# An encoder's attention taken by pairs of heads: softmax weights kept in float32, products with v in two column halves of the array, sums on GpSimd

## The chip, the core and the metric

The kernel runs on one core of a Trainium2 chip. The core has a matrix engine (TensorE, PE in the profile, with its weight loads as PEld), a vector engine (VectorE, DVE), an activation engine (ScalarE, ACT), GpSimd (POOL) and a queue for transfers (SyncE, SP). The metric is device time in microseconds of one execution. Everything is to be computed to float32 accuracy.

## What is computed

Two layers of an encoder over 1024 tokens of 1024 features. The first layer mixes tokens by multi-head latent attention (8 heads) and by retention, side by side, the second by gated linear attention; both end with a gated MLP. The change lies in the attention of the first layer: scores of every head, a softmax over all 1024 keys, and the product with v.

```python
def _mla(cq, ckv, k_rope, positions, q_norm, kv_norm, w_uq, w_ukv, q_head_norm, k_head_norm):
    ...
    scale = MLA_QK ** -0.5                       # 8 heads, 96 columns of q and k, 64 of v
    nb = S // Q_BLOCK
    qb = q.reshape(B, nb, Q_BLOCK, H, MLA_QK).transpose(1, 0, 2, 3, 4)

    def block(qi):
        s = jnp.einsum('bqhd,bkhd->bhqk', qi, k).astype(jnp.float32) * scale
        p = jax.nn.softmax(s, axis=-1).astype(v.dtype)
        return jnp.einsum('bhqk,bkhe->bqhe', p, v)
    ...

for layer in range(DEPTH):                       # DEPTH = 2
    if layer % 2 == 0:
        h = _rmsnorm(x, mix_norm_even[i])
        cq, ckv, k_rope, rq, rk, rv, rg = _split(h @ w_in_even[i], EVEN_SPLIT)
        a = _mla(cq, ckv, k_rope, positions, ...)
        r = _retention(rq, rk, rv, rg, positions, ...)
        x = x + jnp.concatenate([a, r], axis=-1) @ w_out_even[i]
    else:
        ...                                      # gated linear attention
    x = x + _conv_ffn(x, ...)
```

## The kernel before

Work is recorded by Python generators; a scheduling layer then orders each engine's instructions. `weave(main, n, side, m)` steps a main generator and m of n steps of a side one in proportion, and so fixes what lies beside what. A matmul is nearly always a split one: a float32 operand is kept as two float32r parts, hi (a copy on ScalarE) and lo (a subtraction on VectorE, or on GpSimd where `split` is told so), and `mm3` (L346 to L352) issues hi*hi, hi*lo and lo*hi. The matmul line is L349 for all of them. Products that stay in plain float32 (L1385, L811, L1077) are one instruction in the program and two records in the trace.

The attention is the class `Mla`. `produce(pr)` makes q, k and v of a pair of heads from the compressed projections, in 128-token tiles; v is split into hi and lo pages of 128 columns, 64 of v and 64 constants (1.0 in hi, 0.0 in lo), so that one product gives the output and the sum of the weights at once. `prepare(i)` turns q and k of head i to features by tokens, splits them, and finds each query's largest score: 16 matmuls of hi parts (L1440), a maximum on VectorE for each (L1441), and a row that subtracts it. `attend(i)` runs one head: 2 halves of 512 queries by 8 key tiles of 128. A step is one `mm3` for the scores, an exponential on ScalarE (L1469), the split of the weights x into hi and lo (cast on ScalarE, L327, subtraction on VectorE, every second one on GpSimd, L328), and, four steps behind (AHEAD), one `mm3` with the v page into an accumulating PSUM bank. After 8 key tiles ScalarE copies 64 rows of output and VectorE 64 rows of the sum; after the second head of a pair, `y = 1/z` by Ln and Exp with one Newton step, the division, and a DMA to DRAM, from which the output projection reads it back.

The order around it: the retention of the last pair of heads (`ret(3)`) has as its side work the gates, `produce(0)` and `prepare(0)`; then come eight loops of `attend(i)`, with `prepare(i + 1)`, and `produce` of the next pair in the even ones, as side work; in the last two, the operands of the output projection are loaded (`early`) and its first weights (`weights`). PSUM has 8 banks: 5 in the lane "mm" and 3 in the lane "mr", which the side work uses. SBUF pages come in tags with a number of buffers each: "w" has 6 pages of 4 KB, "raw" 2, "hx" 32, "pg" 3.

## Time and profile before

| | |
|---|---|
| median of 3 runs | 2590.84 us (2588.73 to 2591.42) |
| profiled execution | 2591.09 us, span 2589.3 us |
| PE busy | 2551.8 us (99%) |
| DVE busy | 1650.5 us (64%) |
| ACT busy | 1187.7 us (46%) |
| POOL busy | 151.0 us (6%) |

A row of a group gives line, engine, operation, the tiles it writes and reads (`out<-in`), the shape, a count, the busy time in us, the mean of one in ns, and the engine's idle time before them with what ended it. Records of matmuls overlap, since they are pipelined: the time that one costs is read from the starts of successive ones, in a timeline, and not from its length. A shape such as 128*64 128x512 is rows*columns of the array and then partitions x elements of the output. In a timeline the columns are the start, the time until the last of the group ends, engine, line, operation, tiles, shape and count.

### The profile page before, as it was taken

The numbers are of one execution on the slowest core, as the hardware profiler recorded it, in microseconds if no ns is written. First come the engines' busy times: TensorE is split into PE (matmuls) and PEld (weight loads), VectorE is DVE, ScalarE is ACT, GpSimd is POOL, SyncE is SP. The second block draws the span as 40 slices with busy tenths as digits, with TensorE's granted clock in tenths as the row PEclk, the third lists the DMA queues.
The fourth block names the chain that finished last, engine by engine and source line by source line (L and its number), as shares of the span: only waits on it lengthen the run. The fifth ranks groups of instructions, "written<-read, shape, count | busy, mean of one in ns | idle before, by whom it ended". The sixth has DMA issues, their size and how long they took to land.

```text
span 2589.3 us, 33133 instructions
## 1 busy us (share of the span) xinstructions
PE 2551.8 (99%) x12776; PEld 2134.4 (82%) x12776; DVE 1650.5 (64%) x2607; ACT 1187.7 (46%) x2163; POOL 151.0 (6%) x222
## 2 busy tenths in 40 slices
PE   8999999999999999999999999999999999999999
PEld 8889877777888888887888898897788888887887
DVE  6444778778678767676363455648588676775331
ACT  5333667788444333334242445657453333334221
POOL 0000024343000000000000000000000000000000
PEclk9999999999999999999999999999999999999999
DMA  6111100003632222227453211223722222237443
GB/s 193 40 45 42 42 23 12 18 18 122 195 98 73 82 86 85 82 95 262 151 153 106 62 50 45 70 68 108 256 88 75 87 84 82 82 114 254 139 142 92
DMA packets 320596, 253.81 MB, mean 98 GB/s; under 512 B 14828, under 2 KB 271957, under 8 KB 320437
## 3 DMA queue, kind: packets, MB, share of 16 engines
q1 hardware_dynamic: 317877, 243.30, 30.1%
q0 software_dynamic: 2560, 8.39, 0.8%
q8 instruction: 100, 1.64, 0.3%
q14 instruction: 59, 0.48, 0.1%
HBM read 193.71 MB, written 57.93 MB: 97 GB/s over the span
## 4 chain that ended last, share of the span: by engine, by line
PE 71%; DVE 5%; ACT 3%; DMA 3%; issue 1%; SPq 0%; DVEq 0%; ACTq 0%
PE mm L349 65%; DMA st<-d 1%; PE mr L1098 1%; PE mr L349 1%; PE mr L1028 1%; PE mr L1385 1%; DVE hx L328 1%; PE mr L1440 1%; PE mr L1073 1%; PE mr L1387 1%; ACT w L327 1%; DVE sr L1441 0%; DVE xa L1145 0%; DVE hr L998 0%; DVE w L328 0%
## 5 line engine op out<-in xcount | busy, mean ns | idle before, releaser
L349 PE MATMUL mm<-hx,w 128*128 128x512 f32 (+1 forms) x3600 | 869.4, 393 | 1.5 <-ACT hx L1237 1.4
L349 PEld LDWEIGHTS mm<-hx,w 128*128 128x128 f32 (+1 forms) x3600 | 669.9, 187 | 145.4 <-ACT hx L1237 2.2
L328 DVE TENSOR_TENSOR w<-raw,w 128x1024 fp32r<-128x1024 f32 (+2 forms) x271 | 299.3, 1107 | 300.3 <-ACT w L327 284.8
L327 ACT CAST w<-raw 128x1024 fp32r<-128x1024 f32 (+2 forms) x321 | 285.6, 893 | 414.0 <-PE mm L349 351.7
L349 PE MATMUL mm<-w,hx 128*128 128x256 f32 (+1 forms) x2304 | 363.2, 305 | 2.5 <-POOL w L328 1.9
L349 PE MATMUL mm<-h,wf 128*128 128x512 f32 x1368 | 328.9, 389 | 0.0
L349 PEld LDWEIGHTS mm<-w,hx 128*128 128x128 f32 x2304 | 307.3, 191 | 22.6 <-POOL w L328 2.5
L349 PE MATMUL mm<-gh,w 128*128 128x512 f32 x1344 | 316.4, 393 | 4.9 <-ACT gh L327 3.9
L349 PEld LDWEIGHTS mm<-gh,w 128*128 128x128 f32 x1344 | 251.3, 189 | 62.2 <-ACT gh L327 5.6
L349 PEld LDWEIGHTS mm<-h,wf 128*128 128x128 f32 x1368 | 256.8, 188 | 53.3
L1235 DVE TENSOR_TENSOR hx<-mm,hx 128x512 f32<-128x512 f32 x190 | 130.5, 687 | 154.3 <-PE mm L349 154.3
L327 ACT CAST wf<-raw 128x1024 fp32r<-128x1024 f32 x78 | 81.9, 1053 | 187.3 <-DVE raw L1221 118.1
L349 PE MATMUL mm<-hx,wf 128*128 128x512 f32 x552 | 131.9, 389 | 0.0
L349 PEld LDWEIGHTS mm<-hx,wf 128*128 128x128 f32 x552 | 103.6, 188 | 21.5
L349 PE MATMUL mm<-h,w 128*128 128x512 f32 x456 | 109.5, 389 | 0.0
L349 PE MATMUL mm<-hr,hr 128*128 128x512 f32 x336 | 103.8, 402 | 2.3 <-ACT hf L1469 1.7
L328 DVE TENSOR_TENSOR wf<-raw,wf 128x1024 fp32r<-128x1024 f32 x78 | 95.1, 1222 | 12.0 <-ACT wf L327 11.9
L349 PEld LDWEIGHTS mm<-h,w 128*128 128x128 f32 x456 | 85.6, 188 | 17.8
L1265 ACT ACTIVATE pg<-pg 128x1024 f32<-128x1024 f32 x44 | 46.7, 1062 | 106.3 <-DVE pg L1264 105.8
L1264 DVE SCALAR_TENSOR_TENSOR pg<-mm,c,pg 128x512 f32<-128x512 f32 (+1 forms) x100 | 74.0, 746 | 33.0 <-ACT pg L1259 33.0
L349 PE MATMUL mm<-hf,w 128*128 128x512 f32 x384 | 88.8, 392 | 0.0
L349 PEld LDWEIGHTS mm<-hf,w 128*128 128x128 f32 x384 | 72.2, 188 | 16.0
(364 smaller groups left out, 3084.6 us busy)
## 6 DMA issues: line engine op xcount, KB each, us to landing
raw<-in_ffn_w_up SPq DMA_DIRECT2D x88, 512.0 KB
raw<-in_ffn_w_down SPq DMA_DIRECT2D x64, 512.0 KB
st<-d SPq DMA_DIRECT2D x95, 256.0 KB
d<-pg SPq DMA_DIRECT2D x44, 512.0 KB
raw<-in_ffn_w_down SPq DMA_DIRECT2D x32, 384.0 KB
raw<-in_w_in_odd SPq DMA_DIRECT2D x24, 512.0 KB
raw<-in_w_out_even SPq DMA_DIRECT2D x16, 512.0 KB
raw<-in_w_out_odd SPq DMA_DIRECT2D x16, 512.0 KB
```

Of the source, the lines that this page charges most:

```text
L327: self.nc.scalar.copy(hi, src)
L328: return (rest or self.nc.vector).tensor_tensor(lo, src, hi.bitcast(F32), ALU.subtract)
L349: mm = lambda w, x, start, stop: self.nc.tensor.matmul(out, lhsT=w, rhs=x, start=start, stop=stop, skip_group_check=more)
L1028: nc.tensor.matmul(ps[:, n], lhsT=k3[:, t % 4], rhs=vt(t), start=True, stop=True)
L1073: nc.tensor.matmul(p[:, blk(j)], lhsT=kc[:, blk(j)], rhs=qc[:, blk(j)], start=True, stop=True)
L1098: nc.tensor.matmul(ps, lhsT=w[:, blk(t % 4)], rhs=x, start=n == 0, stop=n == len(terms) - 1)
L1235: add = lambda out, x, y: nc.vector.tensor_tensor(out, x, y, ALU.add)
L1264: nc.vector.scalar_tensor_tensor(dst, g[hf][:, src], cw(tap), dst, ALU.mult, ALU.add)
L1265: nc.scalar.activation(cv, cv, AF.Silu)
L1385: nc.tensor.matmul(ps[:, :192], lhsT=e.cq[k][hf][:, blk(t % 4)], rhs=w1[:, k], start=k == 0, stop=k == 2)
L1387: nc.tensor.matmul(ps[:, 256:], lhsT=e.ckv[k][hf][:, blk(t % 4)], rhs=w2[:, k], start=k == 0, stop=k == 1)
L1440: nc.tensor.matmul(ps, lhsT=qs.tok(0, t)[0], rhs=ks.hi[0][hf], start=True, stop=True)
```

## The change

Attention goes by pairs of heads. `attend(pr)` holds both heads in one step: two `mm3` of scores, two exponentials into one page x of 128 x 2 x 512 in float32 (tag "w"), and no split. GpSimd adds x into `acc` in every step but the first of a half. `products` runs four key tiles at a time: for each, two float32 matmuls with 64 columns of v as weights, head 0 into partitions 0 to 63 of a bank and head 1 into 64 to 127, that is, into the two column halves of the array. `divide` sums `acc` over the partitions by two float32 matmuls with 64 columns of ones, two steps after the half's last products, and divides. v is one float32 page without constants. `prepare(1)` moves in front of the loop, beside the retention of the last pair; in the loop of pair p lie `produce(p + 1)`, `prepare(2p + 2)` and `prepare(2p + 3)`; in the last loop the output projection's operands and its first weights. The weights of `produce` move from "w" to "raw" pages, and every second head's split q and k to "hx".

```diff
--- before.py
+++ after.py
@@ -703,7 +703,7 @@
                 yield from g
             for g in each[-2:]:
                 yield next(g)
-            for i, _ in enumerate(many(m.produce(0), m.prepare(0))):
+            for i, _ in enumerate(many(m.produce(0), m.prepare(0), m.prepare(1))):
                 yield
                 if i in RG:
                     yield next(each[RG.index(i) - 2])
@@ -730,20 +730,12 @@
 
         rest = many(mixed(proj_qk(3), norms()), rg(0, 1, 2, 3))
         self.weave(ret(2), 19, islice(rest, W2), W2)
-        self.weave(ret(3), 19, rest, 39 - W2)
-        for i in range(8):
-            side, n = [], 0
-            if i < 7:
-                side.append(self.on((1, 1), m.prepare(i + 1)))
-                n += 13
-            if i % 2 == 0 and i < 6:
-                side.append(self.on((0, 1), m.produce(i // 2 + 1)))
-                n += 10
-            if i >= 6:
-                side.append(self.on((1, 0), many(early(0, 4, 5, 6, 7, 0, 1)) if i == 6 else
-                                    many(early(0, 2), weights(), early(1, 4, 5, 6, 7, 0, 1, 2))))
-                n += 6 if i == 6 else 9
-            self.weave(m.attend(i), 2 * NT - 2 * (i < 6), many(*side), n)
+        self.weave(ret(3), 19, rest, 52 - W2)
+        for p in range(3):
+            side = many(self.on((0, 1), m.produce(p + 1)), *(self.on((1, 1), m.prepare(2 * p + j)) for j in (2, 3)))
+            self.weave(m.attend(p), 2 * NT - 1, side, 36)
+        side = many(early(0, 4, 5, 6, 7, 0, 1, 2), early(1, 4, 5, 6, 7, 0, 1, 2), weights())
+        self.weave(m.attend(3), 2 * NT, self.on((1, 0), side), 15)
         outs = [(o_a[p], None) for p in range(4)] + [(o_r[p], gates[p]) for p in range(4)]
         return outs, *o, w, [], first[0]
 
@@ -1357,13 +1349,13 @@
         self.e, self.nc, self.outs, self.parts = e, e.nc, outs, parts
         self.wq = e.io["mla_w_uq"][0].rearrange("(k p) f -> p k f", p=P)
         self.wkv = e.io["mla_w_ukv"][0].rearrange("(k p) f -> p k f", p=P)
-        self.pair, self.head, self.behind = {}, {}, []
+        self.pair, self.head, self.behind, self.later = {}, {}, [], []
 
     def produce(self, pr):
 
         e, nc = self.e, self.nc
         krr, krs = e.kr
-        w1, w2 = (e.page(s, F32, "w") for s in ([P, 3, 192], [P, 2, 256]))
+        w1, w2 = (e.page(s, F32, "raw") for s in ([P, 3, 192], [P, 2, 256]))
         nc.sync.dma_start(out=w1, in_=self.wq[:, :, blk(pr, 192)])
         nc.sync.dma_start(out=w2, in_=self.wkv[:, :, blk(pr, 256)])
         qp, kp, vp = [], [], []
@@ -1377,9 +1369,8 @@
                 if not c:
                     qp.append(e.page([P, 2, 192], tag="hx"))
                     kp.append(e.page([P, 2, 192], tag="hx"))
-                    vp.append([e.page([P, 2, 2, P], F32R, tag="hx") for _ in range(2)])
-                    for v, x in zip(vp[-1], (1.0, 0.0)):
-                        nc.gpsimd.memset(v[:, :, :, 64:].bitcast(F32), x)
+                if t % 4 == 0:
+                    vp.append(e.page([P, 4, 2, 64], tag="hx"))
                 ps = e.bank()
                 for k in range(3):
                     nc.tensor.matmul(ps[:, :192], lhsT=e.cq[k][hf][:, blk(t % 4)], rhs=w1[:, k], start=k == 0, stop=k == 2)
@@ -1390,7 +1381,7 @@
                     junk = e.half([P, P])
                     nc.scalar.activation(junk[:, :96], ps[:, blk(j, 96)], AF.Square, accum_out=st[:, t % 4, j:j + 1])
                     nc.scalar.activation(junk[:, :64], pk[:, j, :64], AF.Square, accum_out=st[:, t % 4, 2 + j:3 + j])
-                e.split(pk[:, :, 64:], *(v[:, c, :, :64] for v in vp[-1]))
+                nc.scalar.copy(vp[-1][:, t % 4], pk[:, :, 64:])
                 nc.vector.tensor_copy(qp[-1][:, c], ps[:, :192])
                 nc.vector.tensor_copy(heads(kp[-1][:, c], 96)[:, :, :64], pk[:, :, :64])
                 yield
@@ -1418,7 +1409,7 @@
         e, nc = self.e, self.nc
         qp, kp, _ = self.pair[i // 2]
         hc = blk(i % 2, 96)
-        qs, ks = e.new_split(1), e.new_split(1)
+        qs, ks = (e.new_split(1, "hx" if i % 2 else None) for _ in range(2))
         for t in qs.hi[0] + qs.lo[0] + ks.hi[0] + ks.lo[0]:
             nc.gpsimd.memset(t[96:].bitcast(F32), 0.0)
         for hf in range(2):
@@ -1450,57 +1441,67 @@
         self.head[i] = qs, ks
         yield
 
-    def attend(self, i):
+    def attend(self, pr):
 
         e, nc = self.e, self.nc
+        two = [self.head.pop(2 * pr + j) for j in range(2)]
         for hf in range(2):
-            q, pa = qs.half(0, hf), e.bank()
+            acc = e.page([P, 2, H2])
             for kt in range(NT):
...
+                x = e.page([P, 2, H2], F32, "w")
+                for j, (qs, ks) in enumerate(two):
+                    ps = e.bank()
+                    e.mm3(ps, ks.tok(0, kt), qs.half(0, hf), True, True)
+                    nc.scalar.activation(x[:, j], ps, AF.Exp, scale=96 ** -0.5)
+
+                if kt:
+                    nc.gpsimd.tensor_tensor(acc, acc if kt > 1 else self.behind[-1][2], x, ALU.add)
+                self.behind.append((hf, kt, x))
                 if len(self.behind) > AHEAD:
-                    self.product(*self.behind.pop(0))
-                yield
-        while self.behind and i == 7:
-            self.product(*self.behind.pop(0))
-            yield
-
-    def product(self, i, hf, kt, pa, both):
+                    self.products(pr if kt else pr - (not hf), acc if kt else self.acc)
+                if self.later and kt == 2:
+                    self.later.pop()()
+                yield
+            self.acc = acc
+        if pr == 3:
+            self.products(pr, acc)
+            yield
+            self.later.pop()()
+            yield
+
+    def products(self, pr, acc):
+
         e, nc = self.e, self.nc
...
+        for hf, kt, x in [self.behind.pop(0) for _ in range(AHEAD)]:
+            if not kt:
+                self.pa = e.bank()
+            v = self.pair[pr][2][kt // 4]
+            for j in range(2):
+                nc.tensor.matmul(self.pa[blk(j, 64)], lhsT=v[:, kt % 4, j], rhs=x[:, j], start=kt == 0, stop=kt == NT - 1)
         if kt < NT - 1:
             return
...
+        oy = e.page([P, 2, H2])
+        nc.scalar.copy(oy[:, 0], self.pa)
+        self.later.append(lambda: self.divide(pr, hf, acc, oy[:, 0], oy[:, 1]))
+
+    def divide(self, pr, hf, acc, o, y):
+
+        e, nc = self.e, self.nc
+        z, ps = e.half(), e.bank()
+        for j in range(2):
+            nc.tensor.matmul(ps[blk(j, 64)], lhsT=e.ones[:, :64].bitcast(F32), rhs=acc[:, j], start=True, stop=True)
+        nc.scalar.activation(y, ps, AF.Ln)
+        nc.scalar.activation(y, y, AF.Exp, scale=-1.0)
+        nc.vector.scalar_tensor_tensor(z, ps, -1.0, y, ALU.mult, ALU.mult)
+        nc.vector.scalar_tensor_tensor(y, z, 2.0, y, ALU.add, ALU.mult)
+        nc.vector.tensor_tensor(o, o, y, ALU.mult)
+        if not hf:
+            self.outs[pr] = e.waiting()
+        if pr == 3 and not hf:
+            self.parts[pr] = hi, lo = [e.page([P, H2], F32R, "hx") for _ in range(2)]
+            e.split(o, hi, lo)
+        else:
+            nc.sync.dma_start(out=self.outs[pr][hf], in_=o)
 
 
 def encoder(tc, io):
```

In the order of TensorE, before, the second stretch of head 1's maxima (L1440) beside the scores (L349 with hf tiles) and the products with v (L349, w tiles as weights, into mm_3918) of head 0:

```order
L1440 MATMUL mr_4031<-hr_3932,hr_3928 128x512
L349 MATMUL mm_3918<-w_4021,hx_3461 128x512
L349 MATMUL mm_4166<-hf_3646,hf_3648 128x512
L1440 MATMUL mr_4034<-hr_3934,hr_3928 128x512
L349 MATMUL mm_4166<-hf_3647,hf_3648 128x512
L1440 MATMUL mr_4037<-hr_3932,hr_3930 128x512
L349 MATMUL mm_4166<-hf_3646,hf_3649 128x512
L349 MATMUL mm_4216<-hf_3646,hf_3648 128x512
L349 MATMUL mm_3918<-w_4021,hx_3461 128x512
```

Products, scores and maxima are all single matmuls on the whole array, in any mixture.

In the order of TensorE now, the second group of products of the first pair (L1480, 64 rows of mm_4255 each, head 0 and head 1 in turn) and the maxima of the next pair (now L1431):

```order
L1431 MATMUL mr_4369<-hr_4270,hr_4264 128x512
L1480 MATMUL mm_4255<-w_4243,hx_3433 64x512
L1431 MATMUL mr_4372<-hr_4268,hr_4266 128x512
L1431 MATMUL mr_4375<-hr_4270,hr_4266 128x512
L1480 MATMUL mm_4255<-w_4243,hx_3433 64x512
L1480 MATMUL mm_4255<-w_4295,hx_3433 64x512
L1431 MATMUL mr_4378<-hr_4268,hr_4266 128x512
L1431 MATMUL mr_4381<-hr_4270,hr_4266 128x512
L1480 MATMUL mm_4255<-w_4295,hx_3433 64x512
L1480 MATMUL mm_4255<-w_4330,hx_3433 64x512 x2
L1480 MATMUL mm_4255<-w_4354,hx_3433 64x512 x2
L1431 MATMUL mr_4406<-hr_4268,hr_4266 128x512
```

The eight products of a group stand in three runs here, with whole-array matmuls between them; the 128 products and 16 sums over the ones (L1492) make 39 runs in all.

In the order of TensorE before, near the end of the stretch in front of the attention loop: the last gate (L349), the second half of head 0's maxima (L1440) and the retention's matmuls (L848, L830, L831):

```order
L349 MATMUL mm_3783<-hx_182,w_3284 128x512
L349 MATMUL mm_3783<-hx_181,w_3285 128x512
L1440 MATMUL mm_3818<-hf_3648,hf_3646 128x512
L1440 MATMUL mm_3821<-hf_3650,hf_3646 128x512
L848 MATMUL mr_3829<-c_64,hr_3825 128x128 x4
L830 MATMUL mr_3835<-hr_3779,hf_2203 64x128
L1440 MATMUL mm_3845<-hf_3648,hf_3646 128x512
L1440 MATMUL mm_3848<-hf_3650,hf_3646 128x512
```

The gates' last matmuls stand between the first and the second half of head 0's maxima.

In the order of TensorE now, the end of the stretch in front of the attention loop, with the last maxima of head 1 (L1431) and the retention's matmuls (L840, L822 and L823, which were L848, L830 and L831):

```order
L1431 MATMUL mm_3929<-hx_3825,hx_3821 128x512
L1431 MATMUL mm_3952<-hx_3823,hx_3821 128x512
L840 MATMUL mr_3904<-c_64,hr_3900 128x128 x4
L822 MATMUL mr_3910<-hr_3875,hf_2203 64x128
L1431 MATMUL mm_3955<-hx_3825,hx_3821 128x512
L823 MATMUL mr_3910<-hr_3901,hr_3338 64x128
L822 MATMUL mr_3910<-hr_3875,hf_2203 64x128
L823 MATMUL mr_3910<-hr_3901,hr_3338 64x128
L822 MATMUL mr_3910<-hr_3875,hf_2203 64x128
```

The preparation of head 1 has moved here from the attention loop; the gates' matmuls (L349 with hx and w tiles) stand in front of it.

## Rows read from the trace of the kernel before

**Rows 1.** The page's engine table and chain that ended last, shares by engine

```profile
PE 2551.8 (99%) x12776; PEld 2134.4 (82%) x12776; DVE 1650.5 (64%) x2607; ACT 1187.7 (46%) x2163; POOL 151.0 (6%) x222
...
PE 71%; DVE 5%; ACT 3%; DMA 3%; issue 1%; SPq 0%; DVEq 0%; ACTq 0%
```

**Rows 2.** The exponential's line: durations min/median/max in ns, first and last start

```profile
L1469 ACT ACTIVATE raw<-mm x96: 577/599/727, 380.4 to 602.0; 128x512 f32<-128x512 f32 x96
...
L1469 ACT ACTIVATE hf<-mm x32: 581/598/616, 603.2 to 658.8; 128x512 f32<-128x512 f32 x32
```

**Rows 3.** Windows, busy us of each engine: PE, PEld, DVE, ACT, POOL, clock, DMA

```profile
378.00:658.00 280.00, 270.39 (x1293) 218.69 (x1293) 230.22 (x460) 226.25 (x580) 112.19 (x139) 1.00 0.13 40
...
344.00:378.00 34.00, 31.93 (x191) 24.40 (x189) 29.98 (x69) 17.69 (x40) 10.64 (x21) 1.00 0.06 24
```

**Rows 4.** Waits of PE and PEld, 378 to 659 us: total, times, longest

```profile
PE mr L1428 <- DVE hx L1413: 3.8, 4, 1.3
PE mm L349 <- ACT hf L1469: 1.7, 1, 1.7
PE mr L1440 <- DVE sr L1441: 1.6, 4, 0.5
...
PEld mr L1440 <- DVE sr L1441: 4.5, 9, 0.9
```

**Rows 5.** Groups by shape on PE, 370 to 665 us

```profile
L349 PE MATMUL mm<-w,hx 128*128 128x512 f32 x384 | 116.7, 398 | 0.1
...
L1428 PE MATMUL mr<-c,hx 128*96 128x128 f32 x112 | 16.8, 275 | 4.4 <-DVE hx L1413 3.8 <-DVE hx L1407 0.7
...
L1448 PE MATMUL mr<-c,sr 128*1 128x128 f32 x56 | 4.5, 222 | 0.3 <-DVE sr L1443 0.3
```

**Rows 6.** Timeline of PE in the attention, around 571 us

```profile
570.32 0.40 PE L349 MATMUL mm<-hr,hr 128*128 128x512 f32 x1
570.56 0.87 PE L349 MATMUL mm<-w,hx 128*128 128x512 f32 x3
571.26 0.87 PE L349 MATMUL mm<-hr,hr 128*128 128x512 f32 x3
571.96 0.86 PE L349 MATMUL mm<-w,hx 128*128 128x512 f32 x3
```

**Rows 7.** Timeline of PE, plain float32 matmuls of the production

```profile
333.08 1.03 PE L1387 MATMUL mm<-w,hf 128*128 128x256 f32 x4
333.94 0.65 PE L1385 MATMUL mm<-w,hf 128*128 128x192 f32 x3
```

**Rows 8.** Timeline of PE, float32 matmuls of two row halves in turn

```profile
127.56 1.16 PE L811 MATMUL mr<-hr,hr 64*128 64x128 f32 x16
128.65 0.73 PE L349 MATMUL mm<-hx,w 128*128 128x512 f32 x2
```

**Rows 9.** Timeline of PE, a run of half-width tiles in the second layer

```profile
1775.70 0.70 PE L349 MATMUL mm<-hx,w 128*128 128x512 f32 x2
1776.33 0.68 PE L1077 MATMUL mr<-hr 128*64 128x64 f32 x8
1776.94 0.50 PE L349 MATMUL mm<-hx,w 128*128 128x512 f32 x1
```

**Rows 10.** Groups by shape on ACT, 370 to 665 us: casts of the weights

```profile
L327 ACT CAST w<-raw 128x512 fp32r<-128x512 f32 x96 | 59.7, 625 | 5.1 <-PE mm L349 2.9
...
L327 ACT CAST w<-hf 128x512 fp32r<-128x512 f32 x32 | 19.4, 625 | 0.9
```

**Rows 11.** Groups by shape on DVE, 370 to 665 us

```profile
L328 DVE TENSOR_TENSOR w<-raw,w 128x512 fp32r<-128x512 f32 x48 | 39.1, 814 | 11.0 <-ACT w L327 11.0
L328 DVE TENSOR_TENSOR w<-hf,w 128x512 fp32r<-128x512 f32 x24 | 16.3, 696 | 3.9 <-ACT w L327 3.9
L1488 DVE COPY pg<-mm 64x512 f32<-64x512 f32 x16 | 11.1, 693 | 2.8 <-ACT pg L1487 2.4
...
L328 DVE TENSOR_TENSOR hx<-mr,hx 128x128 fp32r<-128x128 f32 x24 | 6.9, 287 | 14.0 <-ACT hx L327 14.0
```

**Rows 12.** Groups by shape on POOL, 340 to 670 us, and 0 to 40 us

```profile
L328 POOL TENSOR_TENSOR w<-raw,w 128x512 fp32r<-128x512 f32 x48 | 65.2, 1359 | 119.3 <-ACT w L327 85.2 <-PE mm L349 13.2 <-issue 10.1
...
L328 POOL TENSOR_TENSOR w<-hf,w 128x512 fp32r<-128x512 f32 x8 | 11.7, 1467 | 18.1 <-ACT w L327 11.9 <-PE mm L349 6.2
...
L328 POOL TENSOR_TENSOR w<-raw,w 128x1024 fp32r<-128x1024 f32 x2 | 4.7, 2372 | 14.6 <-ACT w L327 10.5 <-DMA hf<-in_x 4.1
```

**Rows 13.** Groups by shape on DVE, 344 to 378 us: head 0's preparation

```profile
L1441 DVE TENSOR_REDUCE sm<-mm 128x1 f32<-128x512 f32 x16 | 10.2, 680 | 0.0
...
L332 DVE SCALAR_TENSOR_TENSOR hf<-mm,c,hf 96x512 fp32r<-96x512 f32 x2 | 1.5, 746 | 0.2 <-ACT hf L331 0.2
...
L328 DVE TENSOR_TENSOR hf<-mm,hf 96x512 fp32r<-96x512 f32 x2 | 1.4, 682 | 0.6 <-PE mr L830 0.6
```

33 lines of the change are left out of this document (removed).

## The prediction

> **What bounds the kernel now.** I read the page's engine table and chain first. TensorE is busy for 99% of the span, and it carries 71% of the chain that ended last, where VectorE has 5% and ScalarE 3% [rows 1]. So the time is TensorE's work plus the little that it stands still, and a change counts through these two alone. The change touches two stretches. The attention loop runs from the first softmax exponential (380.4 us) to the last (658.8 us) [rows 2]. The windows show it and the end of the retention before it [rows 3]: from 378 to 658 us TensorE is busy for 270.4 of 280 us and VectorE for 230.2; from 344 to 378 us TensorE for 31.9 of 34 and VectorE for 30.0. Both are nearly full in both. The waits of the first stretch say what ends TensorE's 9.6 us of idle time: VectorE, by the rotated q and k (L1413) and the row maxima (L1441), and once ScalarE's exponential [rows 4]. The granted clock is 1.00 throughout [rows 3], so its level is no term here. The profiled execution took 2591.09 us, 1.8 us beyond its span of 2589.3; the median of the runs is 2590.84, so I add differences to 2591.1.
>
> **Products with v.** Removed: 8 heads x 2 halves x 8 key tiles x 3 = 384 matmuls of 512 columns [rows 5]. Three of them start every 0.70 us [rows 6], 0.233 each: 384 x 0.233 = 89.5 us. Added: 128 float32 products and 16 float32 sums over the ones, each with 64 weight columns, in one or the other column half. No such matmul stands in the trace, so I bound it. A float32 matmul is two records; two of 256 columns take 333.94 - 333.08 = 0.86 us [rows 7], so one of 512 columns takes 0.86 alone. What matters is whether the two halves overlap. The nearest rows are those of the retention scores (L811), which use two row halves: eight float32 matmuls of 128 columns would take 8 x 0.215 = 1.72 us one by one and took 128.65 - 127.56 = 1.09 [rows 8], that is half of it and 0.23 for the start. So a pair costs between 0.86 (full overlap) and 1.72 us (none); I take 0.86, by the row nearest to it.
>
> The order of the changed program does not keep the pairs together: its scheduler puts maxima matmuls (L1431) between the products. The 144 matmuls stand in 39 runs; a run of n that alternates between the halves needs n/2 slots, rounded up, which makes 82 slots, 62 pairs and 20 singles. 82 x 0.86 = 70.5 us. Each run also switches the array to half-width tiles and back. That has a price in the trace: from 1775.70 to 1776.94 us stand two 512-column matmuls (0.47) and eight half-width records of 64 columns (8 x 0.054 = 0.43), so 0.34 us are left over, and the matmul behind lasts 0.50 us where one elsewhere lasts 0.40 [rows 6, 9]. Of 0.34 to 0.44 us a run I take 0.35: 39 x 0.35 = 13.7. Sum 84.2 against 89.5: TensorE gains 5.3 us. With the pairs kept together it would have been 72 slots in 24 runs, 70.3 us; the scheduler's order eats most of the gain.
>
> **What the other engines lose.** ScalarE's 128 casts of the weights go (59.7 + 19.4 us) [rows 10]. VectorE loses 72 subtractions (39.1 + 16.3), 24 for v (6.9) and 16 copies of the denominators (11.1) [rows 11]: 73.4 of 230.2 us. It was the engine that TensorE waited for, so this is the second gain. What remains late is the burst: while TensorE runs eight products VectorE has only three banks of maxima to work off, and then meets 2 x 0.68 us for every pair of maxima matmuls. I let 4 of the 9.6 us of idle time stay. Bounds: all 9.6 gone, or nothing gained.
>
> **GpSimd** gets 56 additions of 128x1024 in place of 56 subtractions of 128x512. Two of that size took 2.37 us each, of 512 columns 1.36 [rows 12]. In the last pair of heads, where nothing else fills TensorE, a half of the queries holds 16 x 0.70 us of scores, two runs of products (2 x 3.8) and one sum (1.2), 20.0 us, and seven additions make 16.6: hidden, through six weight pages. For pairs 0 to 2 the half is longer by the side work. At the very end the sum over the ones waits for the last addition, and the output projection stands behind it in TensorE's queue: the addition ends 1.2 + 2.4 us after the last scores and the last four pairs of products take 3.4, so 0.2 us, or 2.6 with one addition queued. I take 1. The idle term is then 9.6 - 4 - 1 = 4.6 us gained.
>
> **The moved preparation.** Head 1's preparation leaves the attention loop and stands behind head 0's, beside the retention of the last pair. Per head TensorE spends 16 x 0.233 on maxima, 16 transposes of 16.8/112 = 0.15 and 8 small ones of 0.08: 6.7 us [rows 5, 6]. VectorE spends 16 x 0.680 + 1.5 + 1.4 = 13.8 us on it [rows 13]. Attention loses 6.7 us of TensorE time. The stretch in front of it grows by 6.7 us if VectorE can follow and by 13.8 if VectorE is full. It is busy for 30.0 of 34 us there [rows 3], and in the changed order the gates' matmuls are used up before head 1's maxima, so only the retention's small matmuls lie beside them. I let half of VectorE's 4.0 idle us take some of it: 11.8. Net + 5.1 us, between 0 and + 7.1.
>
> The first output weights' DMA is issued on SP ahead of the operands' loads, once the last production has freed its page; it has the whole last pair to land in, so I cost it at nothing. The same holds for the smaller v pages and for production's weights in another page: production's 0.86 us per matmul stays.
>
> **Sum.** - 5.3 - 4.6 + 5.1 = - 4.8: 2591.1 - 4.8 = 2586.3, rounded to 2586 us. Its own range, from the switch price, the moved preparation and the idle time, is 2580 to 2595.
>
> **Rivals.**
> - *The halves do not overlap* (slower). The price is in the column tiles themselves: 144 slots x 0.86 + 13.7 = 137.5 us, 48 more than before; with the other terms 2591.1 + 48 + 0.5 = 2640 us. For it: the trace has no two column halves in turn, its half-width matmuls all use the lower half. Against it: the row halves of L811 overlap fully. It decides once a pair costs over 0.94 us, where the gain of 4.8 is gone. Chance 0.10.
> - *The halves overlap in part*: both halves stream their own 512 columns through the same 128 rows, which the row halves do not. With a quarter of the overlap lost a pair costs 1.075 us: 62 x 0.215 = 13.3, 2600 us. Chance 0.07. The Trainium skill speaks for this one: its page "TensorE: Matmul & The Clock Gate", in the section "Measured speedup vs the span model", gives three column tiles a speedup of 2.38 where full overlap would be 3; no run here shows it so far, and by that ratio a pair would cost about 1.08 us and the kernel about 2600 us, an estimate.
> - *GpSimd sets the pace* (slower): an addition waits for VectorE at a shared port or stands behind the preparation's memsets, weight pages come back late, exponentials and then scores wait. For it: the subtractions on GpSimd ran 1.36 us on average and up to 1.47 in the second group [rows 12], and VectorE's own subtraction 0.81 beside 0.70 us without [rows 11]. Against it: VectorE has a third less to do. It decides from 20.0/7 = 2.9 us an addition. At 3.6 us the last pair loses 2 x 5.3 and the other halves perhaps 5 more: 2602 us. Chance 0.10.
> - *VectorE's relief counts in full*: all 9.6 us of idle time go, and head 1's preparation costs what it saves. 2591.1 - 5.3 - 9.6 = 2576 us. For it: every large wait of rows 4 but one is for VectorE. Against it: the retention stretch is full. Chance 0.15.
>
> **How the numbers follow.** The forecast has 0.58. A measurement of this kernel cannot tell less than about 0.2% from no change, that is 2585.7 to 2596.0 us. The forecast lies near the lower edge: of its 0.58 about 0.27 are faster, 0.29 the same and 0.02 slower. The relief rival adds 0.15 to faster; GpSimd, part overlap and no overlap add 0.25 to slower and 0.02 to the same. So faster 0.42, same 0.31, slower 0.27. The range for 8 in 10 runs from 2574 (below the relief rival) to 2603 (above GpSimd and part overlap); outside stay no overlap and the thin ends.
>
> **What would show it.** L1480's records start in pairs a few ns apart, a new pair of records every 0.43 us; if single records start 0.43 us apart, the overlap is wrong. The product groups then take some 84 us. TensorE's idle time between the first and last exponential falls under 6 us; if L1441 still heads its waits, the relief is wrong. Before the first exponential the page shows VectorE full and TensorE waiting for L1432's maxima; if the first exponential comes only 7 us later, the moved preparation is mis-sized. L1458's additions at 2.4 us and no exponential that waits for POOL; otherwise GpSimd paces. The forecast as a whole is wrong outside 2580 to 2595 us.

## The result and the profile after

The changed kernel takes 2619.6 us (median, 2615.3 to 2621.1) against 2591.1 of the kernel before: ratio 1.0109, 95% interval 1.0093 to 1.0125. The forecast was 2586, range 2574 to 2603: the kernel became slower where I had it faster, and the time lies outside the range. The profiled executions took 2615.3 and 2591.1 us: + 24.2.

The page of the changed kernel, engine table and chain (they answer to [rows 1]):

```profile
PE 2557.1 (98%) x12680; PEld 2087.2 (80%) x12680; DVE 1610.1 (62%) x2487; ACT 1112.1 (43%) x2027; POOL 207.8 (8%) x190
...
PE 87%; DVE 6%; ACT 3%; DMA 2%; issue 1%; POOL 0%; SPq 0%; DVEq 0%; ACTq 0%; POOLq 0%
```

VectorE and ScalarE are relieved as the change meant (40 and 76 us), yet TensorE is busy 5 us longer. Where, the exponential's line says (it answers to [rows 2]):

```profile
L1455 ACT ACTIVATE w<-mm x128: 579/598/726, 403.4 to 679.5; 128x512 f32<-128x512 f32 x128
```

The first exponential comes 23.0 us later than before, and first to last take 276.1 us instead of 278.4. The windows of the changed kernel, columns as in [rows 3]: the front, the loop up to the output projection, and the five stretches between 344 and 687 us in which the granted clock fell:

```profile
344.00:403.40 59.40, 47.97 (x255) 34.16 (x254) 42.41 (x85) 22.52 (x42) 12.74 (x26) 0.89 0.04 15
403.40:687.40 284.00, 261.42 (x1149) 161.43 (x1147) 182.49 (x331) 148.51 (x440) 165.43 (x103) 0.98 0.14 45
353.60:360.40 6.80, 5.56 (x11) 3.28 (x12) 6.22 (x13) 0.58 (x1) 1.86 (x4) 0.50 0.10 39
387.80:394.60 6.80, 6.70 (x21) 4.39 (x21) 6.51 (x14) 0.59 (x1) 0.52 (x1) 0.50 0.00 0
435.50:442.30 6.80, 5.14 (x15) 3.91 (x16) 4.81 (x6) 2.35 (x4) 2.17 (x2) 0.50 0.00 1
636.90:640.30 3.40, 3.39 (x8) 1.40 (x9) 2.66 (x5) 2.29 (x4) 0.00 (x0) 0.50 0.90 293
677.90:681.30 3.40, 3.40 (x9) 1.05 (x9) 2.09 (x1) 2.65 (x5) 3.32 (x2) 0.50 0.59 217
```

In the loop TensorE stands still for 22.6 us (284.0 - 261.4), where it was 9.6, with VectorE only 64% busy instead of 82%. And TensorE now drops to half its clock, 1.2 GHz, after stretches with waits: for 13.6 us in front of the loop (a clock of 0.50 in the first two stretches) and for 13.6 in it (the other three). The kernel before had 1.00 here. The waits of TensorE in the loop (they answer to [rows 4]):

```profile
PE mr L1419 <- DVE hx L1404: 8.0, 6, 1.8
PE mm L349 <- ACT hx L1440: 3.3, 3, 2.4
PE mm L1492 <- POOL pg L1458: 2.7, 1, 2.7
PE mr L1376 <- ACT hf L1382: 2.1, 1, 2.1
```

The largest is not one for the row maxima, as I had expected, but that of the transposes for the rotated q and k (L1404); at the end stands one for the last addition. Why a 0.28 us rotation is late shows in a timeline of the changed kernel (start us, us, engine, line, idle before):

```profile
512.08 3.59 POOL L1458 TENSOR_TENSOR pg<-pg,w 128x1024 f32<-128x1024 f32 x1 [0.26 <-ACT w L1455]
...
514.03 1.78 DVE L1404 TENSOR_TENSOR hx<-hf,hf 128x128 f32<-128x128 f32 x1
...
515.88 0.64 PE L1419 MATMUL mr<-c,hx 128*96 128x128 f32 x4 [1.28 <-DVE hx L1404]
```

The instruction lasts 1.78 us and ends 0.14 us after GpSimd's addition (512.08 + 3.59 = 515.67; 514.03 + 1.78 = 515.81), and TensorE stands still behind it. The addition is itself longer than the usual 2.4 us.

The product groups did better than forecast. In the timeline of TensorE two records are one matmul:

```profile
446.25 1.07 PE L1480 MATMUL mm<-w,hx 128*64 128x512 f32 x2
447.25 0.73 PE L1431 MATMUL mr<-hr,hr 128*128 128x512 f32 x2
447.92 1.08 PE L1480 MATMUL mm<-w,hx 128*64 128x512 f32 x4
448.92 0.73 PE L1431 MATMUL mr<-hr,hr 128*128 128x512 f32 x2
449.58 2.79 PE L1480 MATMUL mm<-w,hx 128*64 128x512 f32 x10
452.31 0.97 PE L1431 MATMUL mr<-hr,hr 128*128 128x512 f32 x3
```

One matmul takes 1.00 us to the next instruction, and so does a pair; five take 2.73 = 3 x 0.86 + 0.15. So the column halves overlap in full, and entering and leaving a run costs 0.15 us.

### The profile page after: what moved, and what is told of

Read it like the earlier page. It is cut to its first block, busy times and chain, and to the rows that moved or that the text cites. A ratio compares the mean times of both kernels' runs of the same rounds, so it can differ in the third digit from the quotient of the medians.

```text
span 2613.5 us, 32591 instructions
## 1 busy us (share of the span) xinstructions
PE 2557.1 (98%) x12680; PEld 2087.2 (80%) x12680; DVE 1610.1 (62%) x2487; ACT 1112.1 (43%) x2027; POOL 207.8 (8%) x190
## 4 chain that ended last, share of the span: by engine, by line
PE 87%; DVE 6%; ACT 3%; DMA 2%; issue 1%; POOL 0%; SPq 0%; DVEq 0%; ACTq 0%; POOLq 0%
PE mm L349 73%; PE mm L1480 2%; PE mr L349 2%; PE mr L1090 1%; PE mr L1431 1%; DMA st<-d 1%; PE mr L840 1%; PE mr L823 1%; PE mr L1020 1%; PE mr L822 1%; PE mr L1376 1%; PE mr L1065 1%; PE mr L854 1%; DVE hx L328 1%; PE mr L1378 0%
## 5 line engine op out<-in xcount | busy, mean ns | idle before, releaser
L349 PE MATMUL mm<-hx,w 128*128 128x512 f32 (+1 forms) x3600 | 869.9, 393 | 1.5 <-ACT hx L1229 1.4
L349 PEld LDWEIGHTS mm<-hx,w 128*128 128x128 f32 (+1 forms) x3600 | 670.4, 188 | 146.7 <-ACT hx L1229 2.2
L328 DVE TENSOR_TENSOR w<-raw,w 128x1024 fp32r<-128x1024 f32 (+2 forms) x223 | 261.8, 1177 | 290.7 <-ACT w L327 271.8
L327 ACT CAST w<-raw 128x1024 fp32r<-128x1024 f32 (+2 forms) x225 | 226.0, 1007 | 418.3 <-PE mm L349 363.7
L349 PE MATMUL mm<-h,wf 128*128 128x512 f32 x1368 | 329.0, 389 | 0.0
L349 PE MATMUL mm<-gh,w 128*128 128x512 f32 x1344 | 314.8, 392 | 2.8 <-ACT gh L327 1.9
L349 PEld LDWEIGHTS mm<-h,wf 128*128 128x128 f32 x1368 | 256.8, 188 | 53.3
L349 PEld LDWEIGHTS mm<-gh,w 128*128 128x128 f32 x1344 | 250.1, 188 | 59.5 <-ACT gh L327 3.3
L349 PE MATMUL mm<-w,hx 128*128 128x256 f32 x1920 | 247.5, 287 | 1.3 <-POOL w L328 0.8
L349 PEld LDWEIGHTS mm<-w,hx 128*128 128x128 f32 x1920 | 236.7, 193 | 4.5 <-POOL w L328 1.2
L349 PE MATMUL mm<-hx,wf 128*128 128x512 f32 x552 | 131.9, 389 | 0.0
L1458 POOL TENSOR_TENSOR pg<-pg,w 128x1024 f32<-128x1024 f32 x48 | 123.6, 2575 | 51.8 <-ACT w L1455 48.5
L349 PEld LDWEIGHTS mm<-hx,wf 128*128 128x128 f32 x552 | 103.6, 188 | 21.5
L349 PE MATMUL mm<-h,w 128*128 128x512 f32 x456 | 109.5, 389 | 0.0
L548 POOL DMA_DIRECT2D d<-xb x16 | 8.8, 549 | 1148.1 <-DVE xb L536 1148.0
L349 PEld LDWEIGHTS mm<-h,w 128*128 128x128 f32 x456 | 85.6, 188 | 17.8
L1455 ACT ACTIVATE w<-mm 128x512 f32<-128x512 f32 x128 | 76.0, 606 | 51.8 <-PE mm L349 50.8
```

The lines of the kernel that those rows point to most:

```text
L327: self.nc.scalar.copy(hi, src)
L328: return (rest or self.nc.vector).tensor_tensor(lo, src, hi.bitcast(F32), ALU.subtract)
L349: mm = lambda w, x, start, stop: self.nc.tensor.matmul(out, lhsT=w, rhs=x, start=start, stop=stop, skip_group_check=more)
L1455: nc.scalar.activation(x[:, j], ps, AF.Exp, scale=96 ** -0.5)
L1458: nc.gpsimd.tensor_tensor(acc, acc if kt > 1 else self.behind[-1][2], x, ALU.add)
```

## The experiments

Three theories. A: the loss is the preparation moved in front of the loop. B: GpSimd's additions hold VectorE's instructions, and TensorE waits behind those. C: bursts of eight products leave the preparation's chains uncovered. Each run has its own ratio to the kernel before.

**moved_alone**, on the kernel before:

```diff
-            for i, _ in enumerate(many(m.produce(0), m.prepare(0))):
+            for i, _ in enumerate(many(m.produce(0), m.prepare(0), m.prepare(1))):
...
-            if i < 7:
+            if 0 < i < 7:
...
```

> The kernel before with one thing of the change: the preparation of head 1 stands behind that of head 0, in front of the attention loop (its q and k in pages of the changed kernel's kind). Theory A (the front stretch carries the loss: 6.7 us of moved TensorE work, some 8 us of waits for VectorE and GpSimd and some 6 us of half clock): first exponential at 400 to 404 us instead of 380.4, a granted clock of 0.5 somewhere between 350 and 400 us, the loop 6 to 7 us shorter; 2604 to 2608 us. The prediction's own term: first exponential 11.8 us later, 2596 us. Theory B and C (the loss is in the loop, by GpSimd's additions or by the bursts of products): 2591 to 2596 us as well.

2605.5 us, 1.0058 (1.0043 to 1.0073). Its exponentials (source rows) and the window of its front:

```profile
L1469 ACT ACTIVATE raw<-mm x96: 576/598/720, 405.2 to 618.2; 128x512 f32<-128x512 f32 x96
...
L1469 ACT ACTIVATE hf<-mm x32: 579/598/615, 619.4 to 674.6; 128x512 f32<-128x512 f32 x32
```

```profile
344.00:405.20 61.20, 50.44 (x250) 35.47 (x249) 42.70 (x83) 22.57 (x42) 12.20 (x25) 0.82 0.07 23
```

The first exponential comes 24.8 us later and the clock falls, with none of the change's arithmetic; first to last exponential take 269.4 us, 9.0 less. So A is worth some 15 us, against the 28.5 between the medians of the changed kernel and of the kernel before, and the prediction's net + 5.1 is refuted.

**no_adds**:

```diff
-                if kt:
-                    nc.gpsimd.tensor_tensor(acc, acc if kt > 1 else self.behind[-1][2], x, ALU.add)
+                if not kt:
+                    nc.gpsimd.memset(acc, 1.0)
```

> The changed kernel without GpSimd's 56 additions: the denominators are set to a constant, so the sums of the weights are left out. Theory B (an addition on GpSimd holds VectorE's instruction that starts beside it until the addition ends, 1.78 us where 0.28 is usual, and TensorE waits for the rotated q and k behind it): the waits of L1419 for L1404 fall from 8.0 us to under 4, the 2.7 us wait for the last addition goes, and with them the half clock after 435 and 677 us; 2604 to 2610 us against 2619.6. Theory C (eight products in a row leave the chains of the preparation uncovered, GpSimd has no part): only the wait at the end goes, 2615 to 2618 us.

2588.9 us, 0.9995 (0.9986 to 1.0004): some 30 us less than the changed kernel, where I expected 10 to 16 of B. The eight products in a row are still there, so C has no part in those 30 us. Its loop as a window, and all that is left of TensorE's waits there:

```profile
404.20:659.80 255.60, 253.90 (x1151) 159.16 (x1149) 145.71 (x332) 148.72 (x440) 28.07 (x53) 1.00 0.14 44
```

```profile
PE mm L349 <- ACT hx L1440: 1.4, 3, 0.5
```

28.4 us of loop go: 20.9 of idle time and 7.5 of busy time, with the clock back at 1.00. The groups of VectorE by shape (count, busy, mean ns) say through what; the changed kernel first, no_adds second:

```profile
L1432 DVE TENSOR_REDUCE sr<-mr 128x1 f32<-128x512 f32 x96 | 60.7, 683 | 16.3 <-PE mr L1431 16.3
L328 DVE TENSOR_TENSOR hf<-hr,hf 128x512 fp32r<-128x512 f32 x7 | 13.3, 1932 | 0.0
...
L1404 DVE TENSOR_TENSOR hx<-hf,hf 128x128 f32<-128x128 f32 x12 | 7.9, 657 | 0.0
```

```profile
L1432 DVE TENSOR_REDUCE sr<-mr 128x1 f32<-128x512 f32 x96 | 60.3, 682 | 16.6 <-PE mr L1431 16.6
...
L328 DVE TENSOR_TENSOR hf<-hr,hf 128x512 fp32r<-128x512 f32 x7 | 4.6, 687 | 0.3 <-ACT hf L327 0.3
...
L1404 DVE TENSOR_TENSOR hx<-hf,hf 128x128 f32<-128x128 f32 x12 | 3.4, 283 | 0.0
```

Instructions with both operands in SBUF (pages hf, hx, hr) last on average up to three times as long beside the additions; the maxima, which read PSUM (mr), do not change at all. In all, VectorE is busy for 36.8 us more in the changed kernel's loop than in that of no_adds (182.5 against 145.7) with the same work.

**clears** asks whether any instruction on GpSimd does this (it leaves out the sums too):

```diff
-                    nc.gpsimd.tensor_tensor(acc, acc if kt > 1 else self.behind[-1][2], x, ALU.add)
+                    for part in (acc, acc, acc[:, 0]):
+                        nc.gpsimd.memset(part, 1.0)
```

> The changed kernel with each of GpSimd's 56 additions replaced by three memsets (128x1024 twice, 128x512 once, about 2.4 us together) into the same page: GpSimd is as busy, but reads nothing; the sums of the weights are left out. If any GpSimd instruction holds VectorE until it ends, pieces of 0.96 us hold it less long: 2600 to 2610 us, with VectorE instructions of two SBUF operands up to 1 us longer. If it takes an instruction that reads its operands from SBUF: no VectorE instruction is lengthened by more than some 0.4 us, 2588 to 2594 us as without additions (2588.9). If GpSimd's busy time or the wait for pages behind it is what counts: 2612 us or more.

2590.0 us, 1.0001 (0.9992 to 1.0010). GpSimd's groups, one of VectorE's, and the window of the loop:

```profile
L1459 POOL MEMSET pg<- 128x1024 f32 x98 | 93.6, 955 | 56.8 <-DMA d<-pg 51.4
L1459 POOL MEMSET pg<- 128x512 f32 x49 | 25.7, 525 | 2.8
...
L1389 DVE TENSOR_SCALAR sm<-sm 128x16 f32<-128x16 f32 x6 | 1.5, 244 | 0.0
```

```profile
403.70:659.30 255.60, 253.89 (x1151) 159.16 (x1149) 146.19 (x332) 148.82 (x440) 141.73 (x194) 1.00 0.14 43
```

GpSimd is busy for 141.7 of 255.6 us (165.4 of 284.0 in the changed kernel), and TensorE loses nothing. So busy time of GpSimd is not enough; of the two kinds tried, only the one that reads SBUF costs time. The Trainium skill states this, on its page "SBUF — State Buffer" in the section "Who interferes with whom": a VectorE instruction with two inputs in SBUF contends with a GpSimd instruction that reads SBUF, and not with one that only writes it, and the port that they share is an exclusive lock. The runs agree: the rotation (L1404) takes 657 ns beside the additions and 283 without, the maxima 683 and 682, and in clears no VectorE instruction with two operands in SBUF lasts more than 0.02 us over its median in no_adds. One with a single operand is held even by the memsets: L1389 takes 244 ns on average beside the memsets, 175 in no_adds and 749 beside the additions.

**half_adds** cuts each addition into one per head:

```diff
-                    nc.gpsimd.tensor_tensor(acc, acc if kt > 1 else self.behind[-1][2], x, ALU.add)
+                    for j in range(2):
+                        nc.gpsimd.tensor_tensor(acc[:, j], (acc if kt > 1 else self.behind[-1][2])[:, j], x[:, j], ALU.add)
```

> The changed kernel with each addition on GpSimd cut into two of 128x512, one for each head: the same work in twice as many instructions. Theory B (VectorE's instruction with two operands in SBUF stands until GpSimd's current one ends): each addition takes 1.3 to 1.4 us instead of 2.4, a VectorE instruction is lengthened by at most some 1.4 us, the waits of L1419 for L1404 fall from 8.0 to 3 or 4 us; 2600 to 2612 us against 2619.6. Rival (GpSimd's total is what counts, whatever its pieces): the additions take 2 x 1.36 = 2.7 us a tile instead of 2.4, 2620 to 2628 us.

2611.8 us (2606.9 to 2617.4), 1.0084 (1.0066 to 1.0103): 8 us under the changed kernel, at the edge of what B gave, with intervals that overlap a little. Two of TensorE's waits in the loop:

```profile
PE mm L1493 <- POOL pg L1459: 4.9, 1, 4.9
...
PE mr L1419 <- DVE hx L1404: 2.6, 5, 1.5
```

The wait for the rotations fell from 8.0 us, as B had it, and the one for the last addition rose from 2.7; two halves take 2 x 1.42 us on GpSimd. It speaks for B; alone it would not decide.

**ahead1** (AHEAD = 4 becomes 1):

> The changed kernel with the products of one key tile issued at every step, instead of four tiles (eight products) at every fourth: AHEAD = 1. Theory C (bursts leave chains uncovered): TensorE's idle time in the loop falls from 22 us by 8 or more, some 25 switches more at 0.35 us and no pair broken cost about 0 to 3 us: 2607 to 2614 us. Theory B (GpSimd holds VectorE): idle time as before, 2619 to 2623 us.

2647.7 us, 1.0225 (1.0208 to 1.0242). TensorE's idle time in the loop is 25.0 us, where C had it fall by 8 or more from 22.6; with no_adds, C is refuted. The group of the products, and the largest wait in the loop:

```profile
L1480 PE MATMUL mm<-w,hx 128*64 128x512 f32 x256 | 97.3, 635 | 0.0
```

```profile
PE mr L1419 <- DVE hx L1404: 14.4, 3, 5.3
```

The products now stand, with the sums, in 87 runs instead of 39; in 45 of them one matmul stands alone, at the price of a pair (100.6 us from the start of a run to the next instruction, waits taken out, against 78.6 in the changed kernel); and the wait for the rotations got longer, not shorter.

**dve_adds** (nc.gpsimd becomes nc.vector) and **mixed_adds**:

```diff
-                    nc.gpsimd.tensor_tensor(acc, acc if kt > 1 else self.behind[-1][2], x, ALU.add)
+                    eng = nc.gpsimd if pr < 3 and kt > 4 - hf else nc.vector
+                    eng.tensor_tensor(acc, acc if kt > 1 else self.behind[-1][2], x, ALU.add)
```

> The changed kernel with the 56 additions on VectorE instead of GpSimd. At 1.2 us each (the 128x1024 subtractions in the trace) VectorE gets 67 us more in the loop and loses what GpSimd's port cost it, some 20 us: 230 of 285 us busy. Theory B: no VectorE instruction is lengthened, the long waits for L1404 go, 2606 to 2616 us. Rival (VectorE's total in the loop is what counts): TensorE waits more for L1432, 2625 us or more.

> The changed kernel with 21 of the 56 additions on GpSimd (pairs 0 to 2, key tiles 5 to 7 of the first half and 4 to 7 of the second, when VectorE mostly reduces maxima out of PSUM) and 35 on VectorE (beside the production's rotations, the division and in the last pair). Theory B: no VectorE instruction of the rotations and the division stands behind GpSimd, and VectorE has 25 us less than with all 56: 2596 to 2604 us, under the 2605.8 of all additions on VectorE. Rival (it is VectorE's own load that costs in that kernel's favour, or GpSimd's in any place): 2606 to 2615 us.

2605.8 us, 1.0062 (1.0047 to 1.0077), and 2599.6 us, 1.0039 (1.0025 to 1.0053). With all additions on VectorE no instruction of it is lengthened, and TensorE waits at the end of a preparation instead; with 21 of the 56 left on GpSimd three rotations are still held for 1.8 us, as many as in the changed kernel, and besides them only two instructions of L490. The first wait of the one, then of the other:

```profile
PE mr L1439 <- DVE sr L1434: 4.9, 3, 1.6
```

```profile
PE mr L1419 <- DVE hx L1404: 4.2, 4, 1.3
```

**The front.** Four runs on the changed kernel: the maxima matmuls of heads 0 and 1 issued twice (twice), the maxima taken by halves of the keys (by_half), the gates later (late_gates), and all three (front_all):

```diff
-RG = 8, 17
+RG = 17, 22
```

```diff
-                nc.tensor.matmul(ps, lhsT=qs.tok(0, t)[0], rhs=ks.hi[0][hf], start=True, stop=True)
+                for _ in range(1 + (i < 2)):
+                    nc.tensor.matmul(ps, lhsT=qs.tok(0, t)[0], rhs=ks.hi[0][hf], start=True, stop=True)
```

```diff
-        for t in range(NT):
-            for hf in range(2):
+        for hf in range(2):
+            for t in range(NT):
...
-            yield
+                if t % 2:
+                    yield
```

> The changed kernel with each maxima matmul of heads 0 and 1 issued twice, the second over the first in the same bank: 32 matmuls of 0.233 us more on TensorE where it waits for VectorE, nothing else. Theory A (in front of the loop the half clock costs some 6 us): less half clock between 387 and 395 us; the one after 353 us comes from a wait for GpSimd and stays; first exponential 0 to 4 us earlier than 403.4, 2615 to 2620 us. Rival (VectorE's maxima set the pace, the clock is a side effect): first exponential at 403 to 405 us, 2619 to 2622 us. Rival (TensorE's own work counts there): 7 us more, 2627 us.

> The changed kernel with the maxima of a head taken for the first half of the keys over all eight query tiles, then for the second half. The second half's k, whose page GpSimd has to clear first, is then needed eight matmuls later. Theory A (waits of TensorE for GpSimd's page, 2.7 us at 352 us, and the half clock that follows): that wait goes and the half clock at 353.6 with it, first exponential 3 to 6 us earlier; 2613 to 2617 us. Rival (VectorE's maxima set the pace of the stretch): first exponential where it was, 2619 to 2621 us.

> The changed kernel with the second halves of the last two gates (24 matmuls each, 5.6 us) placed later in front of the loop: RG = 17, 22 instead of 8, 17, so that the last one stands behind head 0's maxima, where the chain to head 1 runs. Theory A, as by_half and twice leave it (TensorE and VectorE work in turns there: VectorE stands still for 7.2 us at 362 us while TensorE does a gate, TensorE stands still for 1.9 and 1.7 us at 377 and 382 us): first exponential 3 to 7 us earlier than 403.4, 2613 to 2617 us. Rival (the sum of VectorE's work sets the stretch): first exponential within 1 us, 2619 to 2621 us.

> The changed kernel with the three edits in front of the loop together: the gates' halves late (RG = 17, 22), the maxima by halves of the keys, and the maxima matmuls of heads 0 and 1 issued twice. Each alone gave 2 to 3 us. If they take away different waits of one kind (TensorE and VectorE in turns): first exponential 5 to 9 us earlier than 403.4, 2611 to 2615 us. If VectorE's chain of head 0 and then head 1 sets the stretch: first exponential at 401 to 404 us, 2616 to 2619 us.

2617.3 us, 1.0105 (1.0090 to 1.0120); 2617.1 us, 1.0105 (1.0090 to 1.0120); 2616.3 us, 1.0097 (1.0082 to 1.0112); together 2621.0 us, 1.0123 (1.0109 to 1.0136). The 2 to 3 us of the single ones do not add up; none is told from the changed kernel with certainty. The exponentials of front_all and the window of its front:

```profile
L1457 ACT ACTIVATE w<-mm x128: 580/598/726, 405.3 to 682.4; 128x512 f32<-128x512 f32 x128
```

```profile
344.00:405.30 61.30, 51.85 (x280) 38.73 (x281) 43.36 (x87) 22.45 (x43) 11.77 (x25) 0.94 0.04 16
```

The clock is up from 0.89 to 0.94, and the first exponential is no earlier; with the single edits it came at 403.8, 403.7 and 402.4 us, against 403.4. So no one wait sets the front, as the rivals had it. front_all alone does not rule out that the half clock costs time, since its doubled matmuls add 7.5 us of TensorE work; but in the changed kernel VectorE is busy for 12.7 of the 13.6 us at half clock in front of the loop (6.22 + 6.51 in the windows above), so the half clock can have cost little there. The kernel before's window from 344 us to its first exponential:

```profile
344.00:380.40 36.40, 33.75 (x200) 25.65 (x199) 31.34 (x71) 19.26 (x42) 10.64 (x21) 1.00 0.06 23
```

VectorE is busy for 31.3 of 36.4 us there, for 42.4 of 59.4 in the changed kernel: of the 23.0 us it works 11.1 more and stands still 11.9 more. Its largest wait in the changed kernel's front:

```profile
DVE sm L1432 <- PE mm L1431: 9.3, 3, 7.2
```

7.2 us of it in one piece, while TensorE does the last gate and matmuls of the retention. By the records of both engines, both work in 33.0 of these 59.4 us, one alone in 24.3 and neither in 2.1; in the kernel before both work in 30.5 of 36.4 us. So the two work in turns, where I had one of them always at work. An order that avoids it I did not find: late_gates shortened VectorE's largest wait to 5.4 us and brought the first exponential forward by 1.0.

**Pair 0 single.** The kernel before's code for heads 0 and 1, pairs for the rest, with three divisions of the additions: all on GpSimd (first_single), as in mixed_adds (first_single_mixed), and only key tiles 4 to 7 of the second half on GpSimd (single_second, whose edit is shown). single_shared and single_early are single_second with another spread of the preparation:

```diff
-        for p in range(3):
...
+        for i, side, n in ((0, (self.on((1, 1), m.prepare(1)), self.on((0, 1), m.produce(1))), 23),
+                           (1, (self.on((1, 1), m.prepare(2)), self.on((1, 1), m.prepare(3))), 26)):
+            self.weave(m.attend1(i), 2 * NT - 2, many(*side), n)
+        for p in range(1, 3):
...
+                    eng = nc.gpsimd if pr < 3 and hf and kt > 3 else nc.vector
```

> The same with all additions of pairs 1 to 3 on GpSimd, as in the changed kernel. Theories A and B: against 2619.6 the moved preparation's 15.4 us come back, of the additions' 28 us some 8 go with pair 0, and 3.3 us of the products are lost: 2596 to 2602 us. Rival (the two losses hide each other): 2605 us or more.

> Pair 0 as in the kernel before (head after head, weights split on the way, head 1's preparation beside head 0, those of heads 2 and 3 beside head 1), pairs 1 to 3 by pairs as in the changed kernel, with the additions shared by GpSimd and VectorE as in mixed_adds. Theories A and B together: the moved preparation's 15.4 us come back and 3.3 of the 13.4 us of the products are lost; from mixed_adds' 2599.6 that gives 2584 to 2590 us. Rival (VectorE, with two preparations beside head 1, becomes the bound there, 13.8 us more of its work in 35 us): 2595 us or more.

> first_single_mixed with two edits: only key tiles 4 to 7 of the second half of the queries are added on GpSimd (pairs 1 and 2), so that no rotation stands behind it, and three steps of preparation move from beside head 1 to beside head 0. Theory B: the 1.3 us waits of TensorE behind a rotation go (two), and part of the 3.9 us between head 1 and pair 1 with its half clock: 2582 to 2587 us, ahead of before's 2590.6. Rival (VectorE, with 44 additions, becomes the bound of the pairs): 2589 to 2594 us.

> first_single_mixed with one edit: of pairs 1 and 2 only key tiles 4 to 7 of the second half of the queries are added on GpSimd, the other additions on VectorE; the preparation stays where it was. Theory B: TensorE's waits of 1.18 and 1.29 us behind a held rotation go, 2585 to 2587 us. Rival (VectorE's own additions cost as much): 2588 to 2591 us.

> single_second with the side work of pairs 1 and 2 spread over 13 steps instead of 15, so that the next pair's preparation ends before the pair does. If waits at the end of the preparation (0.9 us a time behind the small row copies) cost anything: 2583 to 2586 us. If VectorE is too full to be earlier: 2587 to 2592 us.

first_single 2607.6 us, 1.0068 (1.0051 to 1.0084): 5.6 us over what A and B together gave, and in the rival's range. It is 12.0 us under the changed kernel, which is A's 15.4 less 3.3 for the products, so nothing came back for the additions that went with pair 0. That the two losses hide each other, as the rival had it, is not shown, for GpSimd's subtractions hold VectorE in the single pair too. A rotation there and the subtraction beside it:

```profile
430.99 1.35 DVE L1414 TENSOR_TENSOR hx<-hf,hf 128x128 f32<-128x128 f32 x1
```

```profile
430.71 1.48 POOL L328 TENSOR_TENSOR w<-raw,w 128x512 fp32r<-128x512 f32 x1 [1.07 <-ACT w L327]
```

first_single_mixed 2588.7 us, 0.9993 (0.9983 to 1.0002); single_shared 2588.0, 0.9996 (0.9987 to 1.0005); single_early 2588.0, 0.9996 (0.9988 to 1.0005): no difference from the kernel before. single_second 2586.5 us, 0.9987 (0.9978 to 0.9996): 0.13% under the kernel before, with an interval that only just leaves out 1. It is the best of five versions, and its two neighbours show no difference, so I take none of them for a gain; all but first_single give back the changed kernel's loss. single_shared missed its range (2582 to 2587), and for single_early the second of its two expectations holds (VectorE too full). Its loop as a window, and its two largest waits:

```profile
380.00:659.00 279.00, 271.04 (x1217) 180.75 (x1217) 216.12 (x407) 170.84 (x481) 70.57 (x85) 0.98 0.13 42
```

```profile
PE mm L349 <- DVE w L328: 2.7, 3, 1.4
PE mr L1429 <- DVE hx L1414: 1.8, 1, 1.8
```

Both of them belong to the single pair.

## Why the prediction was wrong

- **Products, - 5.3 forecast: right in kind, too small.** The halves overlap, so the first two rivals fall; the ratio of three column tiles on the Trainium skill's page "TensorE: Matmul & The Clock Gate" (section "Measured speedup vs the span model"), by which the prediction estimated 1.08 us a pair, does not carry over to these two halves (0.86). The switch was mis-sized: 0.15 us a run, not 0.35. In no_adds, at full clock, the 39 runs of products and sums take 76.1 us, from the start of each to the next instruction: - 13.4.
- **GpSimd, "hidden": the step that failed.** Its pace was read rightly (2.35 to 2.41 us for most additions, as [rows 12] had it). I asked only whether an addition is ready in time, not what it does to VectorE while it runs, and put that at nothing. no_adds shows what it costs: some 30 us, of which 20.9 are idle time and 7.5 busy time of TensorE in the loop. My sign for it saw nothing: most additions took 2.4 us and no exponential waited for GpSimd, as forecast. The rival had the shared port, but let only GpSimd wait, which it does as well (3.59 us for the addition above); the loss comes from VectorE's waiting. The trace of before showed it already. The durations of one line of the division (shortest, median, longest, in ns), and one such instruction in the timeline of VectorE, then of GpSimd:

```profile
L1497 DVE SCALAR_TENSOR_TENSOR pg<-pg,pg x8: 677/1629/1672, 451.6 to 666.5; 128x512 f32<-128x512 f32 x8
```

```profile
525.52 1.67 DVE L1497 SCALAR_TENSOR_TENSOR pg<-pg,pg 128x512 f32<-128x512 f32 x1
```

```profile
525.35 1.29 POOL L328 TENSOR_TENSOR w<-raw,w 128x512 fp32r<-128x512 f32 x1 [2.56 <-PE mm L349]
```

  Five of the eight took 1.6 us or more where 0.68 would do, each beside a subtraction on GpSimd. The change made GpSimd's instructions 1.8 times as long (2.4 against 1.36 us).
- **Idle time in the attention, - 4.6 forecast, + 13 measured.** Without the additions 1.7 us are left, that is - 7.9: VectorE's relief is real, and more than I took. The additions turned it round, by the step above.
- **Moved preparation, + 5.1 net forecast, + 15.4 measured** (moved_alone). The loop gave back 9.0 instead of 6.7. The front grew by 23.0 us in the changed kernel and 24.8 in moved_alone, outside my bounds of 6.7 and 13.8. The bounds are the added work of either engine, as if one of them were always at work; in the front they took turns.
- **"The granted clock is 1.00, so its level is no term": wrong.** TensorE's idle time was priced at itself; behind it came 27 us at 1.2 GHz. In the loop that cost about 7 us (busy time 261.4 against 253.9 in no_adds); in the front, where VectorE was busy meanwhile, little.

The sum: front + 11.2 over forecast, idle time + 18, clock + 7, products - 8; that is 28 of the 29 us between - 4.8 and + 24.2. That the moved preparation costs 15.4 us is shown by moved_alone; that it does so by turns rests on traces alone, and which order would have hidden it stays open.

## What to carry to other kernels

An engine with time to spare is not free: before work goes to GpSimd, look at what VectorE does beside it and where its operands lie, and look in the trace for instructions of one line and shape whose longest, or even median, is far above the shortest. Work moved to a stretch where two engines are both nearly full can cost more than the larger of its two parts when they wait for each other: 23 us here, where VectorE's part was at most 13.8. And TensorE's waits can cost more than themselves: among 22.6 us of them the changed loop spent 13.6 us at half clock, among 9.6 us the kernel before spent none.

## What the runs showed of the hardware

- Two float32 matmuls of 128x64 weights and 512 columns in the two column halves take 0.86 us together, the time of one, and a run of them 0.15 us beside that.
- A GpSimd addition of 128x1024 float32 takes 2.4 us and, beside VectorE's own SBUF work, up to 3.6; VectorE's of the same size 1.22 us. 56 of them cost this kernel some 30 us on GpSimd, 17 on VectorE and 11 shared (against no_adds).
- GpSimd's memsets, 0.96 us for 128x1024, lengthened none of VectorE's instructions in the loop of clears by more than 0.4 us, and of those only one line, with a single SBUF operand (L1389).
